# Three sizes of token block in one hybrid decoder step: quarters of 258, a projection moved to the middle, norms from products of x with itself

## The chip, the cores and the metric

One core of a Trainium2 chip runs the whole program. The metric is device time in microseconds (us) of one execution. The engines are PE (TensorE, matmul; PEld is its weight load), DVE (VectorE), ACT (ScalarE), POOL (GpSimd) and SP, whose queue issues every transfer of this kernel.

## The reference

One step of a one-layer hybrid decoder on 1024 prompt tokens and 8 sample tokens, 1032 in all, width 1024, all in float32:

```python
u = rmsnorm(h, norm_mix)
proj = u @ w_in                       # 46 column tiles of 128 and 8 single columns
# RWKV-7 time mixing on one part of proj, gated DeltaNet on another: o_a, o_b
mix = gate_a * (o_a @ w_branch_a) + gate_b * (o_b @ w_branch_b)
h = h + mix @ w_out
u2 = rmsnorm(h, norm_ffn)
h = h + (silu(u2 @ w_ffn_gate) * (u2 @ w_ffn_up)) @ w_ffn_down    # inner width 2816
h = h + sigmoid(rmsnorm(h, norm_ple) @ w_ple_gate) * (pe @ w_ple_proj)   # pe has width 256
y = rmsnorm(h, norm_final)
```

## The kernel before, in words

Everything lies with channels on the 128 partitions and tokens along the free dimension. A float32 product is made of three float32r products: each operand is split into a high and a low half (`xh`, `xl`, `wh`, `wl`), and high·high, high·low and low·high are summed in PSUM (`products`, line 219; line 75 issues each matmul). `weights` (line 190) loads 128x512 pieces of a weight; ACT writes the high half (line 186) and POOL the low half (line 187). A "product" below is one such matmul instruction on PE.

Tokens are cut into three blocks of 344 (`BW`). The stages in order are:

- **Start** (pool `ld`, lines 291 to 401). It loads x (`xs`), the per-layer embeddings (`pes`) and the weights of the per-layer projection (`wps`). `project(m)` makes the eight tiles of pe @ w_ple_proj (144 products) and stores them to `pp_d`. `sums(g)` squares x on ACT and DVE, adds on DVE and POOL and sums over partitions with a float32 product against ones; `inv_rms` (line 269) takes the diagonal, runs a reciprocal square root of 12 small DVE instructions (`rsq`, line 237) and spreads the result R with a float32 product; `scale(g, R)` multiplies `xs` by R and splits it into `xh`, `xl`. PE's order here is the order of the code.
- **The input projection and the two recurrences**. `stream` (line 407) yields the products of the input projection one by one, and `order` (line 112) weaves the recurrences' instructions between them by a model clock.
- **Branches** `wa` and `wb` (lines 1429 to 1461), then the output projection `wo` of the mixer in two parts t: t = 0 is two blocks of 344 tokens, t = 1 two of 172 (`QB`, line 1436). Each result is added to x (tile `H`), stored to `h_d` and squared (`square`, line 1465).
- **mixes(t)** (line 1489) scales H by R (line 1497) and makes seven sums of quarters of the normed input, each split into halves (`ms` line 1507, `xh` line 1509, `xl` line 1510), as the Strassen scheme of the feed-forward needs them.
- **strassen** (line 1543): 22 calls, each with seven products of weight sums, every one on both token parts: 84 matmuls of 344 columns and 84 of 172 a call. After every second pair of calls (one call gives two tiles of gate or up) the down projection `wd` (line 1648) adds to h, which is read from and written back to `h_d`.
- **The end**: gate of the embedding, final norm, store of y, in blocks of 384, 384 and 264 tokens (`EB`).

PSUM has six banks for such accumulators (`acc`), taken in turn. Outside the start and `order`, a scheduler places instructions on every engine by priority; each engine then runs its own list in that order, and SP issues its transfers in order.

Of the kernel before, what the change touches and what calls it, by code (L numbers as in the profile page):

```python
# [58 lines left out]
def hybrid(ctx, tc, a, o):  # L59
# [159 lines left out]
    def products(wh, wl, nk, xh, xl, evac, blocks=range(NBLK), new=None, t0=0):  # L219
        tc.cur_priority += LATER  # L220
        for b in blocks:
            c = cols(b)
            if new:
                new.append(new.pop(0))
                ps = new[-1]()
            else:
                banks.append(banks.pop(0))
                ps = banks[-1].tile([P, width(c)], F32, tag="acc", name="acc")
# [40 lines left out]
    def inv_rms(R, ps, pl_, newps):  # L269
# [7 lines left out]
        tt(e[:, :n], ps, idr[:, :n], MULT)  # L277
        if n >= 2 * P:
            V.tensor_reduce(r[:, 0, 0:2], e[:, 0:2 * P].rearrange("p (i t) -> p i t", t=P), AX.X, ADD)
        for i, c in enumerate(parts):  # L280
            if n < 2 * P or i > 1:
                V.tensor_reduce(r[:, 0, i:i + 1], e[:, c], AX.X, ADD)
# [7 lines left out]

    with tc.tile_pool(name="ld", bufs=1, side="right", reuse_waits="tile") as ld, \
            tc.manual_schedule(engines={mybir.EngineType.PE}):
        xs = ld.tile([P, KT, TOK], F32, name="xs")
        pes = ld.tile([P, 2, TOK], F32, name="pes")
        wps = ld.tile([P, 16, P], F32, name="wps")
        wph, wpl = (ld.tile([P, 16, P], F32R, name=x) for x in ("wph", "wpl"))
        ph, pl = (ld.tile([P, 2, TOK], F32R, name=x) for x in ("ph", "pl"))

        def acc():
            return psd.tile([P, BW], F32, tag="acc", name="acc")  # L300

        spare = [acc, acc, lambda: st1([P, BW]), lambda: psp.tile([P, BW], F32, tag="zp", name="zp")]

        def load_w(m):
            SP.dma_start(wps[:, 2 * m:2 * m + 8].rearrange("p (m k) c -> p m k c", k=2),
                         a["wpp"][m:m + 4].rearrange("m p k c -> p m k c"))

        def load_x(b):
            SP.dma_start(xs[:, :, cols(b)], a["xT"][:, :, cols(b)].rearrange("k p t -> p k t"))
# [4 lines left out]
        load_x(0)  # L314
        load_w(4)
        SP.dma_start(cs, a["const"])
        load_x(1)
        SP.dma_start(vec, a["vec"])
        load_x(2)
        idr = diagonal(ld, BW)  # L320

        own = ld.tile([P, BW], F32, name="own")
        pv = [pes[:, k, cols(b)] for k in range(2) for b in range(NBLK)]
        wv = wps.rearrange("p m c -> p (m c)")
        wv = [wv[:, i * BW:i * BW + BW] for i in range(5)]

        def sums(g):

            sq = (pv + [own], wv + [own], pv)[g]
            for k in range(KT):  # L330
                x, y = xs[:, k, cols(g)], sq[k if k < 4 else 4 + k % (len(sq) - 4)]
                if g == 0 and k in (1, 3, 5):
                    tt(y, x, x, MULT)
                else:
                    act(y, x, AF.Square)
                if k >= 4:
                    (gtt if g or k == 6 else tt)(sq[k - 4], sq[k - 4], y, ADD)
            for k in range(2):
                (gtt if g else tt)(sq[k], sq[k], sq[k + 2], ADD)
            ps = ct([P, BW])  # L340
            for k in range(2):
                mm(ps, ones, sq[k], start=(k == 0), stop=(k == 1))
            return ps

        def inv(g, ps):
            R = ld.tile([P, BW], F32, tag="R0", name="R0", bufs=2)
            tc.cur_priority -= 2 * LATER
            inv_rms(R, ps, ld, ft)
            tc.cur_priority += 2 * LATER
            return R  # L350

        def scale(g, R):
            c = cols(g)
            for k in range(KT):
                (gtt if k % 2 else tt)(xs[:, k, c], xs[:, k, c], R, MULT)
                split(xs[:, k, c], vc("nmix", k), xh[k][:, c], xl[k][:, c])

        def project(m):
            po = ld.tile([P, TOK], F32, tag="po", name="po", bufs=4)

            def evac(b, ps):
                tc.cur_priority -= 3 * LATER
                if b == 1:
                    V.tensor_copy(po[:, cols(b)], ps)
                else:
# [1149 lines left out]
    for t in range(2):  # L1515
# [14 lines left out]
        if t:  # L1530
            astk.close()
# [226 lines left out]
```

## Time and profile before

| what | us |
|---|---|
| timed runs, median of 3 (lowest to highest) | 2151.99 (2151.53 to 2152.81) |
| the profiled execution's own time | 2146.48 |
| its span | 2144.7 |
| PE busy in the span | 2003.7 (93%) |
| DVE, ACT, POOL busy | 1334.3 (62%), 843.2 (39%), 1049.6 (49%) |

PE is busy for nearly all of the span, but matmuls overlap in this profile, so busy says little of the rate: what a product costs is read from the distance between the starts of two neighbours.

### The profile page before, as it was taken

How to read it: one execution, taken by the hardware profiler on the slowest of the kernel's cores; microseconds unless marked ns; L12 is line 12 of the kernel's file. 1: busy time of each engine (PE TensorE's matmuls, PEld its weight loads, DVE VectorE, ACT ScalarE, POOL GpSimd, SP SyncE). 2: the span in 40 equal slices, each digit the busy share in tenths (PEclk: the TensorE clock that was granted, in tenths of full speed). 3: DMA queues.
4: the chain of work that ended last, by engine and by line, in shares of the span. 5: the costliest groups of instructions: out<-in, count | busy, mean ns of one | idle time of the engine just before them, and what ended most of it. 6: DMA issues, size and time to landing. Idle time of an engine off the chain costs nothing.

```text
span 2144.7 us, 40063 instructions
## 1 busy us (share of the span) xinstructions
PE 2003.7 (93%) x14676; PEld 1877.2 (88%) x14676; DVE 1334.3 (62%) x3240; ACT 843.2 (39%) x2068; POOL 1049.6 (49%) x1142
## 2 busy tenths in 40 slices
PE   6998999998999979998899969999999999999996
PEld 5987878777788869898899869999999999999995
DVE  8359766898898279456461785543554535445767
ACT  4333353555554332257232442332413324234532
POOL 5356463566573245730165774544525345354722
PEclk8999999999999999899899969999999999999998
DMA  6334332242343425553555305325143251422322
GB/s 231 119 102 121 112 111 78 92 131 86 102 142 105 133 87 154 164 142 109 189 151 161 110 21 170 107 81 177 45 151 101 69 179 50 140 94 71 124 71 95
DMA packets 214846, 250.86 MB, mean 117 GB/s; under 512 B 47832, under 2 KB 171624, under 8 KB 214648
## 3 DMA queue, kind: packets, MB, share of 16 engines
q1 hardware_dynamic: 214648, 248.29, 37.8%
q8 instruction: 115, 1.88, 0.4%
q14 instruction: 83, 0.68, 0.1%
HBM read 170.82 MB, written 77.40 MB: 116 GB/s over the span
## 4 chain that ended last, share of the span: by engine, by line
PE 68%; DVE 20%; DMA 3%; issue 3%; ACT 3%; POOL 3%; SPq 0%; DVEq 0%; POOLq 0%; ACTq 0%
PE acc L75 59%; PE f L75 3%; PE c L75 2%; DVE GM L738 1%; DVE inv L774 1%; PE zp L75 1%; PE f L79 1%; DVE inv L775 1%; PE s L75 1%; PE x L75 1%; DVE inv L776 1%; DVE L L627 1%; DVE LB L762 1%; DVE H L1497 1%; DMA a<-h_d 1%
## 5 line engine op out<-in xcount | busy, mean ns | idle before, releaser
L75 PE MATMUL acc<-xh,wh 128*128 128x344 f32 (+2 forms) x2360 | 753.1, 320 | 10.5 <-ACT wh L186 6.1
L75 PE MATMUL acc<-xl,wh 128*128 128x344 f32 (+2 forms) x2360 | 751.3, 319 | 6.6 <-DVE xl L1510 6.4
L75 PE MATMUL acc<-xh,wl 128*128 128x344 f32 (+1 forms) x2336 | 746.0, 320 | 1.3 <-POOL wl L187 1.3
L187 POOL TENSOR_TENSOR wl<-ws,wh 128x512 fp32r<-128x512 f32 (+1 forms) x248 | 321.1, 1297 | 463.5 <-ACT wh L186 433.1
L75 PEld LDWEIGHTS acc<-xh,wh 128*128 128x128 f32 (+1 forms) x2360 | 456.1, 193 | 19.1 <-ACT wh L186 6.8
L75 PEld LDWEIGHTS acc<-xl,wh 128*128 128x128 f32 (+1 forms) x2360 | 456.0, 193 | 15.0 <-DVE xl L1510 7.7
L75 PEld LDWEIGHTS acc<-xh,wl 128*128 128x128 f32 x2336 | 453.9, 194 | 7.2 <-POOL wl L187 1.8
L186 ACT ACTIVATE wh<-ws 128x512 fp32r<-128x512 f32 (+1 forms) x248 | 153.7, 622 | 248.5 <-PE acc L75 213.5
L187 POOL TENSOR_TENSOR wl<-s,wh 128x512 fp32r<-128x512 f32 x110 | 142.9, 1300 | 160.9 <-ACT wh L186 160.7
L75 PE MATMUL acc<-hidh,wh 128*128 128x344 f32 x528 | 168.3, 320 | 2.7 <-DVE a L1642 2.6
L75 PE MATMUL acc<-hidl,wh 128*128 128x344 f32 x528 | 169.1, 321 | 0.0
L75 PE MATMUL acc<-hidh,wl 128*128 128x344 f32 x528 | 168.2, 320 | 0.0
L1642 DVE TENSOR_TENSOR a<-a,acc 128x344 f32<-128x344 f32 x120 | 60.8, 511 | 134.0 <-PE acc L75 75.0
L186 ACT ACTIVATE wh<-s 128x512 fp32r<-128x512 f32 x110 | 68.9, 627 | 130.0 <-PE acc L75 110.5
L75 PEld LDWEIGHTS acc<-hidh,wh 128*128 128x128 f32 x528 | 99.0, 188 | 3.6 <-DVE a L1642 3.2
L1600 POOL TENSOR_TENSOR s<-ws 128x512 f32<-128x512 f32 x66 | 86.3, 1307 | 32.5 <-DMA ws<-in_wg 13.7
L75 PEld LDWEIGHTS acc<-hidh,wl 128*128 128x128 f32 x528 | 99.2, 188 | 0.0
L75 PEld LDWEIGHTS acc<-hidl,wh 128*128 128x128 f32 x528 | 99.1, 188 | 0.0
L493 POOL TENSOR_TENSOR cy<-cy,cu 128x344 f32<-128x344 f32 x72 | 69.4, 964 | 50.7 <-ACT cu L492 44.7
L75 PE MATMUL acc<-mxh,wl 128*128 128x344 f32 (+1 forms) x256 | 76.4, 298 | 0.9 <-POOL wl L187 0.9
L1622 DVE TENSOR_TENSOR y<-y,sg 128x344 f32<-128x344 f32 x88 | 75.2, 854 | 3.0
L75 PE MATMUL acc<-mxl,wh 128*128 128x344 f32 (+1 forms) x256 | 76.4, 298 | 0.0
(494 smaller groups left out, 4048.7 us busy)
## 6 DMA issues: line engine op xcount, KB each, us to landing
ws<-in_win SPq DMA_DIRECT2D x92, 256.0 KB, 3.2
a<-h_d SPq DMA_DIRECT2D x120, 172.0 KB, 2.7
h_d<-a SPq DMA_DIRECT2D x120, 172.0 KB, 2.7
pa_d<-gs SPq DMA_DIRECT2D x90, 172.0 KB, 2.1
ws<-in_wg SPq DMA_DIRECT2D x44, 256.0 KB, 2.9
ws<-in_wu SPq DMA_DIRECT2D x44, 256.0 KB, 2.8
ws<-in_wd SPq DMA_DIRECT2D x40, 256.0 KB, 2.6
gate_d<-gs SPq DMA_DIRECT2D x48, 172.0 KB, 2.2
```

The costliest lines, as they stand in the source:

```text
L75: last[0] = TE.matmul(out, w, x, start=start, stop=stop).ins
L79: last[0] = TE.transpose(out, x, ident).ins
L186: act(h, s, AF.Copy)
L187: (eng or gtt)(l, s, h.bitcast(F32), SUB)
L493: gtt(y, y, u, ADD)
L627: V.tensor_tensor_scan(L[:, c * C:c * C + C], ones[:, 0:C], L[:, c * C:c * C + C], 0.0, MULT, ADD)
L738: stt(GM[:, 2 * (c + j) + h], ps[h][:, j], cvf[:, cg, h:h + 1], rwmask, MULT, MULT)
L762: V.transpose(LB[0:32, i0:i0 + 16], G2[:, :, i0:i0 + 16].rearrange("p b i -> p i b"))
L774: tt(u[:, :i], XB[:, :i, :i], LB[:, 16 + i:17 + i, 16:16 + i].to_broadcast([P, i, i]), MULT)
L1600: e(s, A_[p], A_[q], op)
L1622: tt(y, y, sg[i][:, c], MULT)
L1642: tt(y, y, ps, ADD)
```

## The change

Three edits go together. (1) The second half of the layer works on four equal quarters of 258 tokens (`QW`) in place of two blocks of 344 and two of 172: `wb`, `wo`, `mixes` and all Strassen products. (2) The per-layer projection leaves the start and is made after the second part of `wo`, with weights from the common weight path, its embeddings loaded through tile `a`, and each 128x344 result stored on its own from a tile `po` with two buffers. (3) The sums of squares at the start come from float32 products of x with itself (`gram`: a 128x128 block per 128 tokens, of which the diagonal is used). The code of the start stands after `stream` now, so that it can issue the first 144 products of the input projection itself. Pools are placed anew for all this.

```diff
-    def inv_rms(R, ps, pl_, newps):
+    def inv_rms(R, ps, pl_, newps, grams=False):
...
+        if grams:
+            V.memset(r[:, 0], 1.0)
+            for i, c in enumerate(parts):
+                w = slice(0, width(c))
+                tt(e[w, c], ps[w, c], idr[w, c], MULT)
+                V.tensor_reduce(r[w, 0, i:i + 1], e[w, c], AX.X, ADD)
...
-        load_w(0)
-        for b in range(NBLK):
-            SP.dma_start(pes[:, :, cols(b)], a["peT"][:, :, cols(b)].rearrange("k p t -> p k t"))
         load_x(0)
-        load_w(4)
         SP.dma_start(cs, a["const"])
...
+        def gram(g, ps):
+
+            for t0 in range(0, BW, P):
+                w = min(P, BW - t0)
+                for k in range(KT):
+                    x = xs[:, k, g * BW + t0:g * BW + t0 + w]
+                    mm(ps[:w, t0:t0 + w], x, x, start=(k == 0), stop=(k == KT - 1))
+            return ps
...
+        s0 = gram(0, ct([P, BW]))
+        s1 = gram(1, ct([P, BW]))
+        scale(0, inv(0, s0))
+        dense_some(3 * KT)
+        s2 = gram(2, st1([P, BW]))
+        R = inv(1, s1)
+        dense_some(3 * KT)
+        scale(1, R)
+        R = inv(2, s2)
+        dense_some(6 * KT)
+        scale(2, R)
+        dense_some(6 * KT)
...
-    QB = [slice(0, BW), slice(BW, 2 * BW), slice(2 * BW, 5 * BW // 2), slice(5 * BW // 2, TOK)]
-    NT_ = [2 * BW, BW]
+    QW, HW = TOK // 4, TOK // 2
+    QB = [slice(i * QW, i * QW + QW) for i in range(4)]
...
-        dense(a["wb"][m], HB, obh, obl, evac)
+        dense(a["wb"][m], HB, obh, obl, evac, QB)
...
+    mixer_out(0)
+    m0stk.close()
...
+    XM[0] = mixes(xa, 0)
+    for k in range(2):
+        for b in range(NBLK):
+            y = tile("a")
+            SP.dma_start(y, a["peT"][k, :, cols(b)])
+            split(y, None, ph[k][:, cols(b)], pl[k][:, cols(b)])
+    mixer_out(1)
...
+    XM[1] = mixes(xb, 1)
...
+    for m in range(KT):
+        def evac(b, ps, m=m):
+            y = hq[1].tile([P, BW], F32, tag="po", name="po", bufs=2)
+            act(y, ps, AF.Copy)
+            SP.dma_start(pp_d[m, :, cols(b)], y)
+        dense(a["wpp"][m], 2, ph, pl, evac)
...
-            ps = banks[-1].tile([P, width(QB[2 * t])], F32, tag="acc", name="acc")
+            ps = banks[-1].tile([P, QW], F32, tag="acc", name="acc")
```

Three places in the engines' lists show what moved. The first is PE at the very start. Before, PE's list there holds the per-layer projection (`ph`, `pl` on `wph`, `wpl`) with the sums over partitions (`c<-pes,cs`) between:

```order
L75 MATMUL acc_232<-ph_130,wpl_129 128x344
L75 MATMUL c_255<-pes_126,cs_75 128x344 x2
L75 MATMUL acc_259<-ph_130,wph_128 128x344
L75 MATMUL acc_259<-pl_131,wph_128 128x344
L75 MATMUL acc_259<-ph_130,wpl_129 128x344
```

In the change PE's list begins with the products of x with itself (`c<-xs`, `s<-xs`), and the second R (`f_339`) stands behind 24 products of the input projection and the third set of such products:

```order
L75 MATMUL c_138<-xs_125 128x128 x16
L75 MATMUL c_138<-xs_125 88x88 x8
L75 MATMUL c_163<-xs_125 128x128 x16
L75 MATMUL c_163<-xs_125 88x88 x8
L75 MATMUL f_213<-nre_189,cs_75 128x344
L75 MATMUL acc_264<-xh0_101,wh_242 128x344
...
L75 MATMUL acc_264<-xh7_108,wl_249 128x344
L75 MATMUL s_289<-xs_125 128x128 x16
L75 MATMUL s_289<-xs_125 88x88 x8
L75 MATMUL f_339<-nre_315,cs_75 128x344
L75 MATMUL acc_345<-xh0_101,wh_254 128x344
```

So the 144 projection products are gone from here, 72 float32 products came, and input-projection products stand between the norms.

The second place is PE where the mixer's output projection ends. Before, the first Strassen product (`xh00`) follows its last product (`mxh17`) at once:

```order
L75 MATMUL acc_14466<-mxl17_12547,wh_14406 128x172
L75 MATMUL acc_14466<-mxh17_12531,wl_14407 128x172
L75 MATMUL acc_14675<-xh00_13750,wh_14671 128x344
L75 MATMUL acc_14675<-xl00_13757,wh_14671 128x344
L75 MATMUL acc_14675<-xh00_13750,wl_14672 128x344
```

In the change all 144 projection products (`ph`, `pl`) stand between them, and the sums and spreads of the second part's norm (`f<-c`, `f<-nre`) stand among these, 9, 69 and 120 of them in:

```order
L75 MATMUL acc_14456<-mxh17_12322,wl_14396 128x258
L75 MATMUL acc_14648<-ph0_13711,wh_14644 128x344
...
L75 MATMUL f_14430<-c_14428,cs_75 128x258
L75 MATMUL acc_14658<-ph1_13712,wh_14644 128x344
...
L75 MATMUL f_14453<-nre_14433,cs_75 128x258
L75 MATMUL f_14487<-c_14485,cs_75 128x258
L75 MATMUL acc_14776<-ph1_13712,wh_14752 128x344
...
L75 MATMUL acc_14920<-ph1_13712,wl_14897 128x344
L75 MATMUL acc_14944<-xh00_13715,wh_14940 128x258
```

The third place is POOL in the same stretch of the change: the low halves of the first Strassen call's later weights (`wl<-s`) stand behind the first pieces of mixes(1), which need the second part's R (`H10`, `H12` are the scaled tiles):

```order
L187 TENSOR_TENSOR wl_15027<-s_15024,wh_15026 128x512
L1456 TENSOR_TENSOR xl11_14527<-H10_13702,xh11_14520 128x258
L1561 TENSOR_TENSOR s_15069<-ws_14936,ws_14932 128x512
L1456 TENSOR_TENSOR xl11_14527<-H12_13704,xh11_14520 128x258
L187 TENSOR_TENSOR wl_15050<-s_15047,wh_15049 128x512
L1453 TENSOR_TENSOR ms_14545<-H11_13703,H15_13707 128x258
```

From the end of the start stage to the branch products PE's list is the same before and in the change, instruction for instruction.

## Rows read from the trace of the kernel before

**Rows 1.** The profile's page: engines (busy us, share, instructions), TensorE's granted clock in 40 slices, and the chain that ended last, by engine and by line.

```profile
PE 2003.7 (93%) x14676; PEld 1877.2 (88%) x14676; DVE 1334.3 (62%) x3240; ACT 843.2 (39%) x2068; POOL 1049.6 (49%) x1142
...
PEclk8999999999999999899899969999999999999998
...
PE 68%; DVE 20%; DMA 3%; issue 3%; ACT 3%; POOL 3%; SPq 0%; DVEq 0%; POOLq 0%; ACTq 0%
PE acc L75 59%; PE f L75 3%; PE c L75 2%; DVE GM L738 1%; DVE inv L774 1%; PE zp L75 1%; PE f L79 1%; DVE inv L775 1%; PE s L75 1%; PE x L75 1%; DVE inv L776 1%; DVE L L627 1%; DVE LB L762 1%; DVE H L1497 1%; DMA a<-h_d 1%
```

**Rows 2.** Busy time by stage: stretch, its length, busy time and instructions of PE, PEld, DVE, ACT, POOL, then the granted clock (1.00 is 2.4 GHz, 0.50 is 1.2 GHz), DMA share and GB/s. In order: start, input projection with recurrences and `wa`, `wb`, `wo` t = 0, `wo` t = 1, the first two Strassen calls and first `wd`, the other 20 calls with `wd`, the end.

```profile
0.00:59.08 59.08, 36.20 (x160) 31.45 (x161) 51.04 (x98) 30.15 (x67) 31.43 (x36) 0.85 0.60 210
59.08:1074.40 1015.32, 944.23 (x7563) 834.58 (x7563) 701.04 (x1984) 450.51 (x1212) 472.99 (x643) 0.97 0.40 121
1074.40:1119.73 45.33, 45.33 (x291) 45.33 (x289) 29.08 (x46) 15.20 (x31) 34.23 (x31) 1.00 0.48 140
1119.73:1181.60 61.87, 61.87 (x397) 61.67 (x395) 11.17 (x22) 19.41 (x35) 33.29 (x30) 1.00 0.54 162
1181.60:1226.45 44.85, 43.95 (x384) 43.19 (x382) 37.57 (x67) 16.00 (x36) 34.71 (x30) 1.00 0.40 114
1226.45:1344.40 117.95, 93.54 (x515) 87.73 (x513) 81.66 (x161) 44.20 (x109) 77.17 (x81) 0.80 0.33 101
1344.40:2022.50 678.10, 678.10 (x4778) 678.10 (x4779) 336.17 (x666) 229.65 (x503) 322.18 (x255) 1.00 0.34 106
2022.50:2144.70 122.20, 100.47 (x602) 95.10 (x600) 86.55 (x202) 38.09 (x77) 43.59 (x39) 0.93 0.28 90
```

**Rows 3.** PE's instructions in order of time (start us, duration us, engine, line, operation, tiles, shape), first and last of a run: one Strassen round of 24 products begins at 1499.99 with 172 columns, and the next at 1503.22; 1500.07 to 1501.19 is eleven products of 172 columns; 1501.49 to 1503.06 is eleven of 344; 2096.56 to 2098.62 is eighteen of 264 in the end stage.

```profile
1499.99 0.24 PE L75 MATMUL acc<-xh,wh 128*128 128x172 f32 x1
1500.07 0.28 PE L75 MATMUL acc<-xl,wh 128*128 128x172 f32 x1
...
1501.19 0.28 PE L75 MATMUL acc<-xh,wl 128*128 128x172 f32 x1
...
1501.49 0.32 PE L75 MATMUL acc<-xl,wh 128*128 128x344 f32 x1
...
1503.06 0.32 PE L75 MATMUL acc<-xh,wl 128*128 128x344 f32 x1
1503.22 0.24 PE L75 MATMUL acc<-xh,wh 128*128 128x172 f32 x1
...
2096.56 0.28 PE L75 MATMUL acc<-uxh,wh 128*128 128x264 f32 x1
...
2098.62 0.28 PE L75 MATMUL acc<-uxh,wl 128*128 128x264 f32 x1
```

**Rows 4.** The chain that ended last, in order of time (start us, us, what): its longest piece.

```profile
1344.37 678.10 PE acc L75 x4776
```

**Rows 5.** PE in order of time: the first product of `wo` t = 0 and the first of t = 1.

```profile
1119.73 0.32 PE L75 MATMUL acc<-mxh,wh 128*128 128x344 f32 x1
...
1180.15 0.24 PE L75 MATMUL acc<-mxh,wh 128*128 128x172 f32 x1
```

**Rows 6.** The chain that ended last, at the start: x arriving, the first sum of squares' product, and the scaling of a block (`xs`, then the low halves `xl`).

```profile
2.79 8.86 DMA xs<-in_xT
...
19.22 0.86 PE c L75 x2
...
43.20 1.71 DVE xs L355 x4
...
45.33 5.23 DVE xl L254 x8
```

**Rows 7.** PE's groups by form from 0 to 100 us: the products of the input projection (count, busy us, mean ns of one, idle before).

```profile
L75 PE MATMUL acc<-xh,wh 128*128 128x344 f32 x84 | 27.4, 326 | 0.0
L75 PE MATMUL acc<-xl,wh 128*128 128x344 f32 x83 | 27.3, 329 | 0.0
...
L75 PE MATMUL acc<-xh,wl 128*128 128x344 f32 x83 | 26.9, 325 | 0.0
```

**Rows 8.** PE in order of time: two neighbouring runs of float32 products of 128 columns, eight instructions (four products) each.

```profile
942.33 1.06 PE L75 MATMUL x<-S,kc 128*128 128x128 f32 x8
943.22 1.06 PE L75 MATMUL o<-S,q 128*128 128x128 f32 x8
```

**Rows 9.** DVE in order of time at the start: two of the small instructions of the reciprocal square root, about one us apart.

```profile
23.62 0.17 DVE L245 SCALAR_TENSOR_TENSOR nrr<-nrr 128x3 f32<-128x3 f32 x1
...
24.82 0.83 DVE L245 SCALAR_TENSOR_TENSOR nrr<-nrr 128x3 f32<-128x3 f32 x1
```

**Rows 10.** DVE and PE in order of time after the mixer: the scaling of H in mixes(0) and in mixes(1), the last spread of the second part's R (with the idle time before it), and the first product of `wd`.

```profile
1199.01 12.63 DVE L1497 SCALAR_TENSOR_TENSOR H<-H,vec,R 128x688 f32<-128x688 f32 x8
...
1264.62 4.87 DVE L1497 SCALAR_TENSOR_TENSOR H<-H,vec,R 128x344 f32<-128x344 f32 x8 [0.78 <-ACT R L289]
...
1263.29 0.94 PE L75 MATMUL f<-nre,cs 128*128 128x172 f32 x2 [4.68 <-DVE nre L286]
...
1313.02 0.35 PE L75 MATMUL acc<-hidh,wh 128*128 128x344 f32 x1
```

**Rows 11.** ACT in order of time: the copy of one projection result; and the page's transfers: a store of a 128x344 tile (count, KB, us from issue to landing).

```profile
17.42 0.46 ACT L366 ACTIVATE po<-acc 128x344 f32<-128x344 f32 x1 [1.43 <-PE acc L75]
...
pa_d<-gs SPq DMA_DIRECT2D x90, 172.0 KB, 2.1
```

More of the change, by code (lines that the diff above doesn't have):

```diff
@@ L217, in hybrid, with products @@
     banks = [psd]
-    def products(wh, wl, nk, xh, xl, evac, blocks=range(NBLK), new=None, t0=0):
+    def products(wh, wl, nk, xh, xl, evac, blocks=range(NBLK), t0=0):
         tc.cur_priority += LATER
@@ L222, in products @@
             c = cols(b)
[L223 to L228, printed above, removed]
+            banks.append(banks.pop(0))
+            ps = banks[-1].tile([P, width(c)], F32, tag="acc", name="acc")
             for k in range(nk):
@@ L462, in stream, with kvr, load_x, inv @@
                 yield from product(ti, *w, b)
+    def kvr(f):
+        return [4 + f, 8 + f, f]
+    jobs = [12, *kvr(0), 13, *kvr(1), *kvr(2), 18, 19, "b", *kvr(3), 20, 21, 14, 15, 16, 17, 22, 23, 24, 25, 26, 27, 28, 29]
+    dense_in = stream(jobs + list(range(30, 46)))
+    with tc.tile_pool(name="ld", bufs=1, side="right", reuse_waits="tile") as ld, \
+            tc.manual_schedule(engines={mybir.EngineType.PE}):
+        xs = ld.tile([P, KT, TOK], F32, name="xs")
+        def load_x(b):
+            for k in range(0, KT, 4):
+                SP.dma_start(xs[:, k:k + 4, cols(b)], a["xT"][k:k + 4, :, cols(b)].rearrange("k p t -> p k t"))
+        load_x(0)
+        SP.dma_start(cs, a["const"])
+        SP.dma_start(vec, a["vec"])
+        load_x(1)
+        load_x(2)
+        idr = diagonal(ld, BW)
+        def gram(g, ps):
[5 more added lines that the diff above has]
+            return ps
+        def inv(g, ps):
+            R = ld.tile([P, BW], F32, tag="R0", name="R0", bufs=2)
+            tc.cur_priority -= 2 * LATER
+            inv_rms(R, ps, ld, ft, True)
+            tc.cur_priority += 2 * LATER
+            return R
+        def scale(g, R):
+            c = cols(g)
+            for k in range(KT):
+                (gtt if k % 2 else tt)(xs[:, k, c], xs[:, k, c], R, MULT)
+                split(xs[:, k, c], vc("nmix", k), xh[k][:, c], xl[k][:, c])
+        def dense_some(n):
+            for _ in range(n):
+                next(dense_in)
+        s0 = gram(0, ct([P, BW]))
[10 more added lines that the diff above has]
+        dense_some(6 * KT)
+    w0h, a0h, kah, ka1 = vx[:, 0:4], vx[:, 4:8], vx[:, 8:12], vx[:, 12:16]
+    ts(w0h, vc("w0", 0, 4), 0.5, None, MULT)
+    ts(a0h, vc("a0", 0, 4), 0.5, None, MULT)
+    ts(kah, vc("ka", 0, 4), 0.5, None, MULT)
+    ts(ka1, vc("ka", 0, 4), -0.5, 1.0, MULT, ADD)
     def conv(ci):
@@ L1469, in square @@
             return
-        d = tile("c", width(c))
+        d = newd(width(c))
         act(d, src, AF.Square)
@@ L1512, in mixes, with mixer_out @@
         return hi, lo
-    XM = []
-    for t in range(2):
-        qw = width(QB[2 * t])
-        sq = [hq.tile([P, BW], F32, tag=f"sq{i}", name="sq")[:, :qw] for i in range(2)]
+    def mixer_out(t):
+        sq = [hq[t].tile([P, QW], F32, tag=f"sq{i}", name="sq") for i in range(2)]
         for m in range(KT):
             def evac(c, ps, m=m):
-                i = int(c.start > QB[2 * t].start)
-                x = tile("a")[:, :qw]
+                i = c.start // QW % 2
+                x = tile("a")[:, :QW]
                 SP.dma_start(x, a["xT"][m, :, c])
@@ L1555, in new @@
             def new(tag):
-                return sp.tile([P, BW], F32, tag=tag, name=tag)[:, :ps.shape[1]]
+                return sp.tile([P, QW], F32, tag=tag, name=tag)
             if n == 0:
@@ L1624, in hybrid @@
             strassen(a["wg"], f0 + j, gate, f0 + j == 0)
+            if f0 + j == 0:
+                pbs.close()
+                hp = pool(hstk, "hid")
+                hh, hl = pair(hp, "hid", 4)
+                tmp = pool(hstk, "tf", 2)
+                depth[0] = 5
             strassen(a["wu"], f0 + j, up)
@@ L1632, in hybrid @@
             ux = pool(ctx, "ux", 1, "right")
-            uh, ul = pair(ux, "ux", KT)
+            uh, ul = ([xb.tile([P, TOK], F32R, tag=f"x{q}{k}", name=f"ux{q}{k}") for k in range(KT - 1)] for q in "hl")
+            for x, q in ((uh, "h"), (ul, "l")):
+                x.append(ux.tile([P, TOK], F32R, name=f"ux{q}"))
             ac = ux.tile([P, TOK], F32, name="ac")
```

196 lines of the change are left out of this document (47 added, 149 removed).

## The prediction

> **What bounds the kernel now.** I read the page first [rows 1]: PE is busy for 93% of the span and two thirds of the chain that ended last is PE. A busy PE says nothing of its rate, so the next view is the table by stage [rows 2]. In 678 us of Strassen and down projection PE never stops, at full clock, with DVE, ACT and POOL at 50%, 34% and 48%; in the chain these 678 us are one piece [rows 4]. There the rate of PE alone sets the time. Two stretches are of another kind: the start, where DVE is busy for 51 of 59 us and PE for 36, and the 118 us behind the mixer, where PE is busy for 93.5 at a clock of 0.80. There something is late for PE.
>
> What a product costs is the distance between starts [rows 3]: ten steps of 172 columns take 1.12 us, so 112 ns each; ten of 344 take 1.57, so 157 ns; seventeen of 264 take 2.06, so 121 ns. Half the columns cost 71%, so a 172-column product pays for a floor. A round of twelve of each takes 3.23 us [rows 3].
>
> **Part 1: quarters of 258.** The columns stay the same; 258 has no row of its own. From 264 and 344, 80 columns are 36 ns, so six columns less than 264 are 2.7 ns and 258 columns should follow every 118.3 ns. The bounds are the floor (112) and the 264 row itself (121). A round of 24 takes 24 x 0.1183 = 2.84 us in place of 3.23, a call of seven rounds 19.9 in place of 22.6. For the 20 calls in the saturated stretch that is 20 x 2.73 = **55 us** gained (bounds 46 and 76 from 121 and 112 ns). What hides the other engines' work remains: even in 622 us in place of 678 DVE would be at 54%.
>
> `wo` t = 0 runs from 1119.73 to 1180.15 [rows 5], 60.4 us for 384 products at 157 ns. 384 of 118.3 ns are 45.4: **15 us** gained (14 to 17). Its second part grows (384 x 112 ns to 45.4); that is counted in part 2's stretch.
>
> `wb` has 288 products of 344 before, 384 of 258 after: 45.2 against 45.4 us. Its POOL, at 34 of 45 us [rows 2], gets one more fixed cost per weight tile, and its tile `c` has two buffers for a chain over DVE, POOL, ACT and DVE that now comes every 1.42 us. I take a **loss of 2** (0 to 6).
>
> The Trainium skill (TensorE: Matmul & The Clock Gate, section Back-to-back issue gap) gives a warm distance of columns / 2.4 GHz + 2.5 ns: 110 ns for 258 columns. It would give 146 for 344, where the trace has 157 [rows 3], so I go by the trace. By an estimate from that section of the Trainium skill, part 1 would gain about 30 us more (3744 products x 8.3 ns), which comes near rival C.
>
> **Part 2: the projection behind the mixer.** It takes 144 products from the start and adds 144 x 157 ns = 22.6 us of PE behind `wo`, with 16 weight pieces for ACT and POOL, 6 loads through tile `a`, 24 copies on ACT and 24 stores. Before, the stretch from the second part of `wo` to the first `wd` product, 1180.15 to 1313.02, takes 132.9 us [rows 5, 10]. Without waits it would now take 45.4 for `wo`, 22.6 for the projection and 2 x 19.9 for two Strassen calls: 108 us. So the projection has room, if it falls where PE waits now.
>
> It does only in part. The second part's R needs two float32 sums and spreads that stand among the projection products, the last behind 120 of 144, so R comes some 21 us after `wo`. Then DVE scales eight tiles of 516 columns, 4.87 x 516 / 344 = 7 us [rows 10], or 9.5 by the first part's row (12.63 x 516 / 688), where POOL is busy too. On POOL the low halves of the first call's last weights stand behind the first pieces of mixes(1) and wait with them for the scaled tiles; PE gets to them later than that, so they cost nothing. POOL then makes half of mixes(1) between the weights' low halves. It is the engine that fills up here, 77 of 118 us before [rows 2] and now with half again as many columns in mixes(1); I put 33 to 40 us on it. On `wo`'s start as zero: R at 67, last piece of mixes(1) at 107 to 110, then one whole call of 20: 128 us, 20 of them waits. That is a **gain of 5** (from a loss of 12 to a gain of 20, the last if POOL keeps up).
>
> The tile `po` has two buffers; a copy of 0.46 and a store of 2.1 [rows 11] make one result every 1.3 to 1.4 us, where PE makes one every 0.94 (six products). Six banks soften it, and the rest falls into the wait for mixes(1): late there is POOL, not PE. If that cover is gone, it costs up to 24 x 0.45 = 11 us.
>
> **Part 3: the start.** Before, the products of the input projection begin at 59.1 us, but 250 are done by 100 us [rows 7], so PE's effective start is 100 - 250 x 0.157 = 60.8. What makes it late is on the chain [rows 6]: x lands at 11.65, behind 1.6 MB of embeddings and weights; the sum reaches PE at 19.2; x is first scaled at 43.2. In between DVE copies projection results and runs small instructions of 0.17 us that take 0.83 while POOL works [rows 9].
>
> After, x is first in the queue. By the share of bytes (1.4 of 3.0 MB in 11.65 us, with the first latency) block 0 lands at about 6.5. A set of 24 products of x with itself costs 24 x 0.222 = 5.3 us at full clock ([rows 8]: eight instructions, four products, in 0.89), twice that at half. With part of it at half clock set 0 ends at 13.5, set 1 at 19; R of block 0 (DVE, 5 us) lies beside set 1 and comes at 20. Scaling and eight low halves (1.7 + 5.2, [rows 6]) end at 28, set 2 at 34, R of block 1 at 36, its scaling and R of block 2 at 49.5. By then 48 input products are done and nothing holds the rest: start 49.5 - 48 x 0.157 = 42, and 2 more for low clock: 44. **Gain 17** (8 if all sets run at half clock, and all small instructions at 0.83; 26 if none do). Behind it PE's list is the same, so the recurrences shift as a whole.
>
> **Sum.** 55 + 15 - 2 + 5 + 17 = 90 us. The profiled execution took 2146.5, so 2056.5 by its own time. The timed runs' median lies 5.5 above it; I subtract from that: 2152.0 - 90 = **2062 us**.
>
> **Rivals.**
>
> B, the move takes the place of the wait: the projection is fully visible, `po` holds it to the pace of its stores, and mixes(1) still ends late. Then the stretch loses 15 in place of winning 5, with PE at half clock in the gaps, as its 0.80 shows [rows 2]: 2082. For it: POOL's list and the late R. Against: that stretch has 45 us beyond its products' time now (132.9 - 384 x 0.112 - 2 x 22.6), and the move needs 22.6.
>
> C, 258 columns come down to the floor that 172 shows, 112 ns: the 20 calls gain 76 in place of 55, the two parts of `wo` 2.4 more each, the first two calls 2: 2062 - 21 - 7 = 2034. For it: 172 and 258 would share one limit. Against: 264 at 121. By the rule of the Trainium skill named in part 1 it would be about the same; the trace at 344 does not agree with that rule.
>
> D, the change doesn't do what it says: a 258-column product costs the mean of the old pair, 134.5 ns. Then Strassen gains nothing, `wo` 106.7 - 768 x 0.1345 = 3, `wb` loses 6, 17 of the start remain, and the stretch behind the mixer comes out even: 2138. Against it stands the 264 row.
>
> E, slower: PE falls to the half clock inside Strassen, because every accumulator is now handed over at one pace of 1.42 us, and an engine behind PE misses it. At half a product takes 0.237 us and a call 39.8 in place of 19.9; 90 us are gone when 4.5 of 22 calls run so, and with six it is 2181. For it: the clock of 0.80 where PE waits now. Against: 1.00 for 678 us with no other engine above 50% [rows 2].
>
> **How the numbers follow.** The forecast gets 0.66, with 2044 to 2082 as its own range from the part bounds. B gets 0.15, C 0.10, D 0.05, E 0.04. The predicted time is the forecast's; 2032 to 2094 takes in B and C and leaves out D, E and the ends of the bounds. About 0.2% (4 us) is what a measurement here can tell from no change. Faster: the forecast, B, C and 0.03 of D, 0.94; same 0.02, the rest of D; slower 0.04, E.
>
> **What would show it.** Right: 258-column products 118 ns apart; the long saturated piece near 622 us at clock 1.00; input products dense from about 50 us; the products of `ph` running without a gap behind `wo`, then waits on POOL or on mixes(1) in the first call's second half. Wrong: distances of 112 or 134 ns; PE idle before DVE's or ACT's evacuation inside later calls; projection products more than 1.3 us per result; the first input products after 55 us.

## The result, and the profile after

The changed kernel takes **2084.64 us** (median of 4 runs, 2083.20 to 2094.33), the kernel before on the same chip 2152.40 (2151.53 to 2160.09): a ratio of 0.969, 95% interval 0.965 to 0.972. That is 68 us less, where 90 were forecast; 2084.6 lies in the range of 2032 to 2094 and just outside the forecast's own one, 2044 to 2082. The profiled execution took 2085.75, 60.7 less than the 2146.5 of the one before, which lay 5.9 under the median of 2152.40. The terms are therefore compared trace with trace, against 60.7.

From the page of the changed kernel, what answers to [rows 1]:

```profile
span 2084.0 us, 40641 instructions
PE 1943.8 (93%) x14904; PEld 1819.6 (87%) x14904; DVE 1321.5 (63%) x3253; ACT 845.0 (41%) x2069; POOL 1045.1 (50%) x1144
PEclk8999899999999999999899998999999999999998
PE 64%; DVE 21%; DMA 4%; ACT 4%; issue 4%; POOL 3%; SPq 0%; DVEq 0%; POOLq 0%; ACTq 0%
```

The same table by stage as [rows 2], at the changed kernel's own cuts: the start up to the first dense input products, recurrences and `wa`, `wb`, the two parts of `wo`, the stretch up to the end of the first `wd`, the dense Strassen calls, the end. Columns as there.

```profile
core 0: us, PE busy (x) PEld busy (x) DVE busy (x) ACT busy (x) POOL busy (x), PEclk, DMA share, GB/s
0.00:53.02 53.02, 30.40 (x198) 27.94 (x199) 32.65 (x95) 14.75 (x27) 18.66 (x22) 0.82 0.41 141
53.02:1070.53 1017.51, 942.45 (x7514) 833.28 (x7513) 702.60 (x1975) 447.33 (x1207) 473.90 (x643) 0.96 0.40 119
1070.53:1116.45 45.92, 45.92 (x386) 45.92 (x385) 30.77 (x62) 17.01 (x38) 33.70 (x39) 1.00 0.49 138
1116.45:1162.53 46.08, 46.08 (x387) 46.08 (x386) 9.05 (x20) 17.19 (x33) 30.14 (x30) 1.00 0.65 188
1162.53:1212.34 49.81, 48.22 (x396) 47.82 (x395) 38.33 (x78) 22.55 (x54) 35.96 (x36) 1.00 0.55 158
1212.34:1331.61 119.27, 99.13 (x634) 92.63 (x632) 84.53 (x157) 50.20 (x127) 72.19 (x75) 0.93 0.42 132
1331.61:1962.22 630.61, 630.57 (x4800) 630.36 (x4801) 337.81 (x666) 237.20 (x507) 336.43 (x264) 1.00 0.38 117
1962.22:2083.98 121.76, 101.04 (x604) 95.61 (x602) 85.71 (x202) 38.79 (x79) 44.11 (x39) 0.92 0.26 82
```

Laid beside the start times of the same products before, the 60.7 us divide so ("at 100 us" is the start of the 250th input product, 99.95 before and 87.12 after):

| term | forecast | measured | from |
|---|---|---|---|
| start, at 100 us | 17 | 12.8 | 99.95 - 87.12 |
| the same, at the first `wb` product | 17 | 3.9 | 1074.45 - 1070.53 |
| `wb` | -2 | -0.6 | 45.3 to 45.9 |
| `wo`, first part | 15 | 14.3 | 60.4 to 46.1 |
| second part of `wo` to first `wd` product | 5 | -7.1 | 132.9 to 139.9 |
| first group of `wd` | 0 | -2.8 | 26.3 to 29.1 |
| Strassen and `wd` behind it | 55 | 52.3 | 682.9 to 630.6 |
| the end | 0 | 0.7 | 122.4 to 121.8 |

Two terms are far off, and both are stretches in which PE waits: of the start's gain 8.9 us are gone before the recurrences end, and the stretch behind `wo`'s first part lost 10 (with the first `wd`) in place of winning 5. The experiments are for these two, and for what part 1 is worth alone.

### The profile page after: what moved, and what is told of

Read it like the earlier page. It is cut to its first block, busy times and chain, and to the rows that moved or that the text cites. A ratio compares the mean times of both kernels' runs of the same rounds, so it can differ in the third digit from the quotient of the medians.

```text
span 2084.0 us, 40641 instructions
## 1 busy us (share of the span) xinstructions
PE 1943.8 (93%) x14904; PEld 1819.6 (87%) x14904; DVE 1321.5 (63%) x3253; ACT 845.0 (41%) x2069; POOL 1045.1 (50%) x1144
## 4 chain that ended last, share of the span: by engine, by line
PE 64%; DVE 21%; DMA 4%; ACT 4%; issue 4%; POOL 3%; SPq 0%; DVEq 0%; POOLq 0%; ACTq 0%
PE acc L75 54%; PE c L75 3%; PE f L75 3%; DVE GM L685 1%; PE zp L75 1%; DVE inv L721 1%; PE f L79 1%; PE s L75 1%; DVE L L574 1%; PE x L75 1%; DVE H L1443 1%; DMA a<-h_d 1%; DVE inv L722 1%; DVE LB L709 1%; DMA out_gdns<-St 1%
## 5 line engine op out<-in xcount | busy, mean ns | idle before, releaser
L75 PE MATMUL acc<-xh,wh 128*128 128x258 f32 (+2 forms) x2360 | 733.3, 311 | 13.1 <-ACT gs L328 5.7
L75 PE MATMUL acc<-xl,wh 128*128 128x258 f32 (+2 forms) x2360 | 728.0, 309 | 9.7 <-DVE xl L250 5.6
L75 PE MATMUL acc<-xh,wl 128*128 128x258 f32 (+1 forms) x2336 | 722.9, 310 | 0.0
L187 POOL TENSOR_TENSOR wl<-ws,wh 128x512 fp32r<-128x512 f32 (+1 forms) x256 | 334.7, 1309 | 440.2 <-ACT wh L186 408.3
L75 PEld LDWEIGHTS acc<-xh,wh 128*128 128x128 f32 (+1 forms) x2360 | 450.7, 191 | 22.8 <-ACT gs L328 6.0
L75 PEld LDWEIGHTS acc<-xl,wh 128*128 128x128 f32 (+1 forms) x2360 | 451.2, 191 | 18.3 <-DVE xl L250 6.4
L75 PEld LDWEIGHTS acc<-xh,wl 128*128 128x128 f32 x2336 | 448.5, 192 | 5.8 <-POOL wl L187 0.5
L445 POOL TENSOR_TENSOR cy<-cy,cu 128x344 f32<-128x344 f32 x72 | 68.8, 955 | 50.2 <-ACT cu L444 44.1
L75 PE MATMUL acc<-mxh,wh 128*128 128x258 f32 x256 | 72.7, 284 | 0.0
L75 PE MATMUL acc<-mxl,wh 128*128 128x258 f32 x256 | 72.6, 284 | 0.0
L75 PE MATMUL acc<-mxh,wl 128*128 128x258 f32 x256 | 72.2, 282 | 0.0
```

Source lines behind the costliest of these rows:

```text
L75: last[0] = TE.matmul(out, w, x, start=start, stop=stop).ins
L187: (eng or gtt)(l, s, h.bitcast(F32), SUB)
L445: gtt(y, y, u, ADD)
```

## Experiments

**The place where the head start is lost.** Comparing the starts of the same instructions in the two traces shows that it is lost at one spot: PE is 13.6 us ahead of before at 185 us and 4.6 ahead at 260. The first line is PE's longest wait there in the changed kernel, the second that of before (who waits for whom: us in total, times, longest).

```profile
PE acc L75 <- ACT gs L328: 5.7, 1, 5.7
```

```profile
PE acc L75 <- ACT gs L440: 1.5, 1, 1.5
```

ACT's own rows there (start, duration, operation, names; in brackets its idle time and who ended it; `...` where rows are left out), first of the changed kernel, then of the kernel before:

```profile
196.90 0.62 ACT L707 COPY inv<-GM 32x512 f32<-32x512 f32 x1 [4.60 <-DVE inv L741]
197.54 0.63 ACT L586 ACTIVATE d<-KR 128x512 f32<-128x512 f32 x1
198.08 0.61 ACT L186 ACTIVATE wh<-ws 128x512 fp32r<-128x512 f32 x1
198.60 0.61 ACT L586 ACTIVATE d<-KR 128x512 f32<-128x512 f32 x1
202.21 0.23 ACT L623 ACTIVATE Gc<-L 128x16 f32<-128x16 f32 x1 [3.00 <-DVE L L574]
202.35 0.61 ACT L186 ACTIVATE wh<-ws 128x512 fp32r<-128x512 f32 x1
202.87 0.78 ACT L328 ACTIVATE gs<-acc 128x344 f32<-128x344 f32 x2
```

```profile
207.97 0.62 ACT L760 COPY inv<-GM 32x512 f32<-32x512 f32 x1 [3.41 <-DVE inv L794]
208.49 0.44 ACT L440 ACTIVATE gs<-acc 128x344 f32<-128x344 f32 x1
...
211.25 0.43 ACT L440 ACTIVATE gs<-acc 128x344 f32<-128x344 f32 x1
212.83 0.63 ACT L639 ACTIVATE d<-KR 128x512 f32<-128x512 f32 x1 [1.15 <-POOL k L634]
217.75 0.23 ACT L676 ACTIVATE Gc<-L 128x16 f32<-128x16 f32 x1 [4.28 <-DVE L L627]
```

The copies `gs` free the two accumulators of the input projection. Before, both stand ahead of `Gc`, the exponential that needs the last of sixteen scans on DVE. In the changed kernel `Gc` stands first, and PE's accumulators wait behind it for DVE. PE's list is the same in both; ACT's and DVE's are not: the scheduler has placed them otherwise. Then the clock adds its part (windows of the changed kernel, columns as above): it is 0.82 over the wait, 0.50 over the next 7.6 us and 0.59 over the 9 behind them, although PE is busy all through both.

```profile
197.65:203.36 5.71, 0.04 (x2) 0.00 (x1) 5.68 (x12) 2.71 (x7) 2.39 (x4) 0.82 0.03 7
203.36:211.00 7.64, 7.64 (x54) 6.84 (x55) 4.92 (x11) 0.88 (x2) 4.72 (x8) 0.50 0.65 194
211.00:220.00 9.00, 9.00 (x78) 8.57 (x78) 4.25 (x11) 2.84 (x5) 0.59 (x3) 0.59 0.09 27
```

Two runs separate this order from the rival that the recurrences swallow any head start. One holds `Gc` back:

```diff
-        act(Gc, ch(L[:, :T])[:, :, C - 1], AF.Exp)
+        late(act(Gc, ch(L[:, :T])[:, :, C - 1], AF.Exp))
```

> The changed kernel with one line more: the activation that makes Gc is held behind the products issued so far, so that ACT's copies of the accumulators stand ahead of it. Theory A (order): PE's wait of 5.7 us at 197 us and the half clock behind it go, 8 to 9 us, and the head start of 13 us reaches the end of the recurrences as 11 to 13: total 2074 to 2077. Theory B (absorbed): the wait shows up at the next place, total 2083 to 2086.

Measured: 2078.63 us, ratio to before 0.966 (0.962 to 0.969); a little above what was expected, and its interval overlaps the changed kernel's, so the times alone would not carry it. The trace does: the two copies run at 196.57, with no `Gc` ahead, and PE's wait for them is 2.4 us in place of 5.7 (the row of ACT, then PE's wait, as above).

```profile
196.57 0.78 ACT L328 ACTIVATE gs<-acc 128x344 f32<-128x344 f32 x2
```

```profile
PE acc L75 <- ACT gs L328: 2.4, 1, 2.4
```

The other keeps the squares in the new start, on the engines of before. ACT's order at `Gc` is then that of before too:

```diff
...
-                    mm(ps[:w, t0:t0 + w], x, x, start=(k == 0), stop=(k == KT - 1))
...
+            for k in range(KT):
+                x, y = xs[:, k, cols(g)], sq[k if k < 4 else 4 + k % 2]
+                if g == 0 and k in (1, 3, 5):
+                    tt(y, x, x, MULT)
+                else:
+                    act(y, x, AF.Square)
+                if k >= 4:
+                    (gtt if g or k == 6 else tt)(sq[k - 4], sq[k - 4], y, ADD)
...
+            for k in range(2):
+                mm(ps, ones, sq[k], start=(k == 0), stop=(k == 1))
...
```

> The changed kernel, but the mean squares are formed as before (squares on ACT, DVE and POOL, then two products with ones); x is still first in the queue and the projection still behind the mixer. In this kernel ACT's order at the second feature of the recurrences is that of before: the copies of input products (gs) stand ahead of Gc, which waits for sixteen scans on DVE. Theory A (order): the head start of the input products over before, whatever it is (I expect 8 to 11 us), is kept to within 4 us until the end of the recurrences, where the changed kernel kept 4 of 13; total 2078 to 2083. Theory B (the recurrences absorb a head start): 2 to 5 us are left there whatever the start does, and the total is 2084 to 2087.

Measured: 2098.05 us (0.975, 0.971 to 0.979): slower than the changed kernel, which neither theory said. Its head start at 100 us is 6.7, so the products of x with itself are worth 6 us at the start. At the spot of `Gc` theory A holds: 1.5 us lost in place of 9. Behind it another 8.6 went, which theory A excluded. The table below sets this beside all runs, as PE's lead over the profiled execution before (us):

| run | `Gc` | 100 us | 185 | 260 to 300 | first `wb` product |
|---|---|---|---|---|---|
| changed kernel | ahead | 12.8 | 13.6 | 4.6 | 3.9 |
| changed kernel again | ahead | 13.1 | 14.2 | 5.1 | 0.9 |
| without projection | ahead | 11.5 | 12.8 | 3.5 | -8.3 |
| without projection, 2nd | ahead | 12.9 | 14.0 | 4.9 | 6.9 |
| embedding later | ahead | 13.1 | 14.0 | 4.9 | 5.3 |
| mixes on DVE | ahead | 12.6 | 13.3 | 3.3 | 4.4 |
| `Gc` behind | behind | 13.1 | 16.7 | 12.6 | 10.8 |
| products first | behind | 22.8 | 23.9 | 19.8 | 15.9 |
| three places | behind | 22.6 | 25.5 | 22.1 | 6.9 |
| squares kept | behind | 6.7 | 7.1 | 5.6 | -3.0 |
| quarters alone | behind | 0.6 | 0.6 | -0.6 | -14.0 |

Between 185 and 260 the six runs with `Gc` ahead all lose 9.0 to 10.0, the five with it behind 1.2 to 4.1. The difference is the order's price, and it repeats. The one line of `Gc` behind is worth 8.0 at 260 us (12.6 in place of 4.6); 3.1 of that are there at 185 already; the line also holds back an earlier `Gc`, before 140 us. What happens from 260 us on does not go by the kernel: the first six rows have the same instructions up to `wb`, in the same order but for a few neighbours, and between 260 us and there they lose anything from -2.0 to 11.8. The second run of the changed kernel was for this:

> The changed kernel itself, once more, for two things: as the yardstick for the run below on the same chip, and to see how far two executions of one program lie apart in the recurrences. If the 12.7 us by which the changed kernel and the one without the projection differ at the end of the recurrences, with the same instructions up to there, are chance, this profile should show its own value there, somewhere between 1023 and 1036, and the same times as before (within 1 us) up to 220 us, the loss of 9 at 190 to 215 included. Total 2083 to 2087, times the ratio of the chips.

Measured: 2089.47 us, before on that chip 2155.51 (ratio 0.968, 0.965 to 0.972). The lead up to 260 us repeats within 0.6, and at the end of the recurrences it is 3.0 lower. With the other five of the first six rows, which end from -8.3 to 6.9, a profile-to-profile difference of some 10 us in the recurrences is chance. The low time of the profiled execution before may be chance too: on this chip alone eleven runs of it lie from 2149.08 to 2171.17.

**The start.** In the changed kernel the R of block 1 is spread at 40.01, 24 products run, and then PE stands for 7.68 us before the spread of block 2's R, although DVE makes block 1's low halves between 45.3 and 50.2 (start, duration, operation, names, count):

```profile
4.98 12.44 PE L75 MATMUL c<-xs 128*128 128x128 f32 x96 [4.98 <-DMA xs<-in_xT]
22.16 0.65 PE L75 MATMUL acc<-xh,wh 128*128 128x344 f32 x1 [4.13 <-ACT xh L249]
35.19 4.98 PE L75 MATMUL s<-xs 128*128 128x128 f32 x48
40.01 0.78 PE L75 MATMUL f<-nre,cs 128*128 128x344 f32 x2
52.22 1.51 PE L75 MATMUL f<-nre,cs 128*128 128x344 f32 x2 [7.68 <-DVE nre L290]
```

The next run, on top of `Gc` behind, puts all three sets ahead and the third spread behind 48 input products (the line of `Gc` is left out here):

```diff
-        scale(0, inv(0, s0))
-        dense_some(3 * KT)
+        R = inv(0, s0)
         s2 = gram(2, st1([P, BW]))
-        R = inv(1, s1)
-        dense_some(3 * KT)
-        scale(1, R)
+        R1 = inv(1, s1)
+        scale(0, R)
+        dense_some(6 * KT)
         R = inv(2, s2)
+        scale(1, R1)
```

> The kernel with Gc held behind, and at the start all three sets of products of x with itself stand ahead of the input products, and the third spread of R behind 48 of them. The wait of 7.7 us at 44.4 (PE for the R of block 2, whose spread stands in PE's order ahead of block 1's products) should go: theory A: block 1's products start at 43 to 46 in place of 53, the head start over the kernel before is 18 to 21 us at 100 us in place of 13, and as the order at Gc passes it on, the total is 2070 to 2074, against 2078.6 with Gc alone. Theory F (DVE is what is late): DVE's small instructions of the second R ahead of the scaling of block 0 only delay the first product (22.2) by 4 to 6, the head start stays at 12 to 14, total 2077 to 2080.

Measured: 2079.05 us, before on that chip 2157.95 (0.965, 0.961 to 0.968). The lead at 100 us is 22.8, more than expected, although the first product starts at 35.8 in place of 22.2: PE's wait is now one of 13.1 us, ahead of the first product. 15.9 of the lead reach `wb`. So theory A's lead came, but the times do not confirm it: by the ratio this run cannot be told from `Gc` behind alone.

**Part 1 alone.** The kernel before with four quarters; projection and squares stay at the start.

```diff
-    QB = [slice(0, BW), slice(BW, 2 * BW), slice(2 * BW, 5 * BW // 2), slice(5 * BW // 2, TOK)]
-    NT_ = [2 * BW, BW]
+    QW, HW = TOK // 4, TOK // 2
+    QB = [slice(i * QW, i * QW + QW) for i in range(4)]
+    NT_ = [HW, HW]
...
```

> The kernel before with part 1 alone: four quarters of 258 columns in wb, wo and the Strassen calls; the projection and the squares stay at the start. From the two traces, part 1 is 52.0 us in the 20 Strassen calls, 14.4 in wo t = 0, a loss of 0.6 in wb and of about 3 in the second part of wo: together 63, so about 2089 against 2152, with 258-column products 120 ns apart and the start and the recurrences as before. If the parts hinder each other less than that, and the junction behind wo gains here what the projection took from it, it is nearer 2083 and the changed kernel's other two parts are worth nothing or less. If the quarters only pay together with the moved projection, it is above 2100.

Measured: 2094.06 us (0.973, 0.968 to 0.978), 59 less: between the first and the third expectation, nearest the first. By the medians part 1 is seven eighths of the whole change (59 of 68); the two intervals overlap, so what parts 2 and 3 add is not shown. The traces, leaving out the recurrences behind 260 us where chance rules, give them nothing: at 260 us the changed kernel is 5.2 us ahead of the quarters alone, and from `wb` to the end it takes 8.7 more. The stretch from the second part of `wo` to the first `wd` product alone is 130.4 us in the quarters alone, 9.5 less than the changed kernel's.

**The stretch behind the mixer.** Two runs leave the projection out (its 144 products and 16 weight pieces; 24 copies of the embedding are stored instead). In the first the copies came ahead of mixes(0) on ACT, in the second where the projection's copies stood.

```diff
-        def evac(b, ps, m=m):
+        for b in range(NBLK):
...
-            act(y, ps, AF.Copy)
+            act(y, ph[m % 2][:, cols(b)].bitcast(F32), AF.Copy)
             SP.dma_start(pp_d[m, :, cols(b)], y)
-        dense(a["wpp"][m], 2, ph, pl, evac)
```

> The changed kernel without the projection behind the mixer: its 144 products, 16 weight pieces and 8 weight loads are left out, and the 24 tiles that are stored are copies of the embedding instead. Theory C (the late R): with no products ahead of them the two spreads of R come some 10 us after wo instead of 31, mixes(1) ends 15 to 20 us earlier, and the stretch from the second part of wo to the first wd product takes 115 to 122 us in place of 140: total 2060 to 2068. Theory D (POOL): POOL is the limit there, mixes(0) alone keeps it until 1234 us, and the stretch takes 130 to 136: total 2074 to 2080. Fully hidden would be 140 and no change.

> As the run without the projection (its 144 products, 16 weight pieces and 8 weight loads left out, copies of the embedding stored in place of its results), but the 24 copies on ACT now stand among mixes(1), where the projection's copies stood; in the first such run they came ahead of mixes(0), which started at 27.5 us on the zero of wo's second part in place of 22.6. Theory H (the projection is hidden behind mixes): the stretch from the second part of wo to the first wd product takes 136 to 140 us, as with the projection. Theory C (late R by the projection): 115 to 130. In between, at 130 to 136, POOL's 16 weight pieces are what it costs.

Measured: 2086.47 us for the first, with the stretch at 139.9, as with the projection; 2079.06 (one run, before beside it 2160.89) and 136.5 for the second. The R of the second part does not come earlier without the projection: its last spread is 85.7 and 82.6 us behind the start of `wo`'s second part, with it 79.4. The stretch repeats well: in the changed kernel, its second run and the three other runs that leave this stage alone it is 139.8 to 140.2. So 22.6 us of products cost 3.4 us there: nearly all of them are hidden, as theory H has it, and theory C falls.

The other neighbour of R is the embedding: its six loads and splits stand ahead of the second part of `wo`.

```diff
-    for k in range(2):
...
-            split(y, None, ph[k][:, cols(b)], pl[k][:, cols(b)])
+    def load_pe():
+        for k in range(2):
...
+                split(y, None, ph[k][:, cols(b)], pl[k][:, cols(b)])
     mixer_out(1)
+    load_pe()
```

> The changed kernel, but the six loads and splits of the embedding stand behind the second part of wo in the program in place of ahead of it. Theory C (they delay R): the spreads of the first part's R come at 9 and 18 us on the zero of wo's second part, as in the run with the quarters alone, in place of 13 and 22; its scaling and mixes(0) start 4 us earlier, and all behind them too: the stretch from the second part of wo to the first wd product takes 134 to 136 us in place of 140, total 2078 to 2081. Theory D (POOL and DVE are full until R of the second part anyway): the stretch stays at 138 to 141, total 2083 to 2086.

Measured: 2080.45 us (0.965, 0.962 to 0.967) and a stretch of 134.5: theory C's numbers. The first part's spreads come at 9.1 and 17.6 us, mixes(0) starts 4 us earlier. The trace carries this; the ratio's interval overlaps the changed kernel's. This stretch is only 4.1 above that of the quarters alone, with the whole projection in it.

What is left is the size of mixes(1). The windows from the scaling of the second part to its last low half, each cut to within 0.9 us, of the kernel before, the quarters alone and the changed kernel (the first number behind the window is its length; then PE, PEld, DVE, ACT, POOL):

```profile
1263.80:1291.20 27.40, 22.82 (x100) 21.64 (x98) 22.01 (x42) 14.67 (x42) 22.93 (x30) 0.58 0.05 14
```

```profile
1258.00:1296.50 38.50, 24.88 (x147) 23.66 (x147) 29.41 (x42) 17.46 (x45) 30.69 (x33) 0.69 0.15 44
```

```profile
1242.72:1285.60 42.88, 34.51 (x225) 31.71 (x224) 35.21 (x49) 23.70 (x60) 37.49 (x37) 0.84 0.23 74
```

Half of the tokens in place of a third: from the start of the scaling to the end of the last low half, 27.1 us become 38.3 with part 1 alone, and 43.5 beside the projection. The last run asks whether POOL is the limit:

```diff
-                e, e2 = (gtt, tt) if k % 2 else (tt, gtt)
+                e, e2 = (tt, tt) if t else (gtt, tt) if k % 2 else (tt, gtt)
```

> The changed kernel, with all 48 sums and low halves of mixes(1) on DVE; POOL keeps the weights' low halves alone. Theory D (POOL fills up, as the prediction has it): mixes(1), 37 us from the scaling to its last piece, is done in 25 to 30 (48 of 0.41 to 0.5 us), the stretch from the second part of wo to the first wd product takes 128 to 133 us in place of 140, total 2073 to 2079. Theory E (DVE is as full as POOL, and its instructions are slowed by POOL's anyway): 48 pieces of 0.7 to 0.9 us take 40 or more, the stretch 142 to 150, total 2087 to 2095.

Measured: 2084.82 us (0.966, 0.964 to 0.969) and 138.9: neither theory. The same window is 40.8 long, and POOL is free for more than half of it, but DVE is busy for nearly all of it:

```profile
1242.40:1283.20 40.80, 32.07 (x217) 29.32 (x216) 40.53 (x72) 23.79 (x60) 17.62 (x12) 0.92 0.23 77
```

So it is not POOL alone: with POOL's share on DVE, mixes(1) takes 41.2 us in place of 43.5, and DVE is what fills up.

**All three places together**: `Gc` behind, products first, embedding later.

> The changed kernel with Gc held behind the products, the three sets of products of x with itself ahead of the input products, and the loads and splits of the embedding behind the second part of wo. If the three places are independent of each other, 8 to 9 us at Gc, 9 to 10 at the start and 5.4 in the stretch behind wo's first part add up: profile to profile 19 to 24 less than the changed kernel, 2060 to 2068 by its own time. If the recurrences take part of it back, as the run with the three sets first showed it (22.8 us of head start at 100 us, 15.9 at the end), it is 14 to 18: 2067 to 2071. If nothing of it reaches the end it is above 2078.

Measured: 2074.52 us (6 runs, 2063.63 to 2081.61) beside the changed kernel's 2089.47 (6 runs, 2081.33 to 2092.83) on the same chip: 15 less by the medians, which is the second expectation's difference; 0.962 of before (0.958 to 0.965). It is faster than both kernels. The expectation counted profile with profile, and there it is only 8.5 less: the profiled execution, 2079.8 of span, was the longest of the six, and 15 us of its lead went between 260 us and `wb`. The stretch behind the mixer takes 136.8 us, so the later embedding wins 3.1 there in place of 5.4; why is open.

## Why the prediction was right and where it was wrong

**Part 1: right, its price a little low.** Behind the first `wd` the Strassen calls take 80.64 us for four (20.16 each, 19.9 predicted), before 90.42: 9.78 gained for four, 49 for twenty. Another 3.1 come from waits in the first group before (93.9 in place of 90.4). In a row 258 columns follow each other every 118.9 ns, 27 steps in 3.21 us:

```profile
1400.01 0.28 PE L75 MATMUL acc<-xh,wh 128*128 128x258 f32 x1
...
1403.22 0.28 PE L75 MATMUL acc<-xh,wh 128*128 128x258 f32 x1
```

The line through 264 and 344 gave 118.3. Over a call, with the steps from one accumulator to the next, it is 120.0; by that the twenty calls lost 5.7 of the 55, and the waits gave 3.1 back. Rivals C and D are out. The 110 ns by the Trainium skill (TensorE: Matmul & The Clock Gate, section Back-to-back issue gap) were not reached: the trace decides, as it did at 344. That section of the Trainium skill gives the formula for a product on its own, without a budget for its weight load; here every product loads its weights. Rival E did not happen: the 630 us run at clock 1.00. `wo`'s first part (14.3 for 15) and `wb` (-0.6 for -2) are as forecast.

**Part 2: the step that failed is that R comes some 21 us after `wo`, because its sums and spreads stand among the projection products.** On `wo`'s start as zero it came at 79.4 in place of 67: `wo`'s second part took 49.6 us in place of 45.4, and R came 30 us after it, as late or later without the projection. These 12 us are the miss; behind R the forecast holds (60.5 us from R to the first `wd` product, 61 forecast). The rows of PE show a chain in place of the projection, with the row of DVE that makes the second sum's input at the end:

```profile
1216.65 0.70 PE L75 MATMUL f<-c,cs 128*128 128x258 f32 x2 [2.89 <-DVE c L1428]
1231.13 0.70 PE L75 MATMUL f<-nre,cs 128*128 128x258 f32 x2 [2.55 <-DVE nre L290]
1231.67 0.65 PE L75 MATMUL f<-c,cs 128*128 128x258 f32 x2
1241.67 0.60 PE L75 MATMUL f<-nre,cs 128*128 128x258 f32 x2
```

```profile
1218.56 0.50 DVE L1428 TENSOR_TENSOR c<-c,sq 128x258 f32<-128x258 f32 x1 [0.77 <-ACT c L1420]
```

The first spread comes 14.5 us behind its sum: DVE runs the instructions for it among pieces of mixes(0), which last until 72 us on the same zero, and they take 12.1 us from first to last. The second sum's input was ready at 1219.1, but the sum stands behind that spread in PE's list. Its instructions on DVE wait for the last piece of mixes(0) and then take 5.2 us with no such piece between. That this order sets R is read from the trace; no run changes it. The trace before could have warned: with no projection there, R's last spread came 37 us after `wo` [rows 2, 10]. Mixes(1) was sized right (33 to 40, measured 37 behind the scaling), but not POOL alone fills up there: DVE does too. Its growth with the larger second part is a price of part 1, whose stretch won only 2.5 us by itself. The six loads and splits of the embedding, counted but costed at nothing, took 3.1 to 5.4.

`po` did not set a pace of 1.3 to 1.4 us per result. The 24 results take 35.4 us, more than the 1.3 us each that the prediction named as a sign of being wrong, but 13 of the 23 steps from result to result are 0.94 to 0.96, and only 3.2 us are waits for `po`; 5.5 are waits for the sums and spreads of R:

```profile
PE acc L75 <- ACT po L1498: 3.2, 2, 1.6
PE f L75 <- DVE c L1428: 2.9, 1, 2.9
PE f L75 <- DVE nre L290: 2.6, 1, 2.6
```

Rival B's time is near the measured one, but not by its mechanism: its projection was to be fully visible, and 3.4 of 22.6 are.

**Part 3: the start was 4 us short, and the step that failed is "PE's list is the same, so the recurrences shift as a whole".** R of block 1 was ready on DVE at 33.9, before the 36 forecast, but its spread stood behind 24 input products and the third set and ran at 40.0. R of block 2 then came at 52.2 in place of 49.5, and the spread itself and the low clock took the rest: the 250th product is at 87.1, an effective start of 47.9 in place of 44. Then 9.0 us were lost at `Gc`, from 13.6 ahead at 185 us to 4.6 at 260. PE's list is the same; ACT's is not, and that could be read before the run from the order in which the two kernels place `gs` and `Gc`.

**Sum.** 90 - 13.1 (start and recurrences) - 14.9 (stretch and first `wd`) - 2.7 (Strassen) + 1.4 (`wb`, the end and `wo` together) gives the 60.7 of the traces. The runs' medians give 7 more, because the profiled execution before lay 5.9 under its median and that of the changed kernel 1.1 above its own. Part 1 carries the result; parts 2 and 3, forecast at 22, left nothing that can be told from chance. Whether the losses from 260 us on also hold an order's effect stays open: the chance of single executions there is larger than any difference left.

## What to carry to other kernels

A head start on one engine can be lost where another engine's in-order list has changed; compare the lists of the engines that free the bottleneck's buffers, not the bottleneck's own alone. Where a later stage has two parts, making them equal lengthens the second part's preparation (here 27.1 to 38.3 us), so part sizes have a price on both sides. To place work into a wait costs little when what ends the wait runs on other engines (3.4 us for 144 products here), but the small steps that come with it (six loads and splits, 3.1 to 5.4 us) can cost as much.

## What was unexpected of the hardware

PE can stay at the low clock while the profile shows it busy without a gap, for a length that differs from one execution to the next. The window 890 to 935 us of the quarters alone, the first run without the projection, and `Gc` behind (columns as above):

```profile
890.00:935.00 45.00, 45.00 (x419) 36.88 (x415) 7.07 (x23) 10.16 (x18) 23.37 (x31) 0.63 0.47 123
```

```profile
890.00:935.00 45.00, 45.00 (x496) 37.82 (x496) 10.00 (x30) 12.65 (x25) 27.82 (x37) 0.82 0.62 147
```

```profile
890.00:935.00 45.00, 43.74 (x435) 40.40 (x432) 17.33 (x61) 19.70 (x65) 25.52 (x33) 1.00 0.61 179
```

The granted clock is 0.63, 0.82 and 1.00, with PE busy for 45.0, 45.0 and 43.7 of 45 us. With 0.63 in the first, most of the window is at the lower level of 1.2 GHz, and between 865 and 950 us that run lost 10.1 us of its lead, while `Gc` behind won 4.8. The changed kernel, with the same instructions there as the run without the projection, has 0.96 in this window with PE busy for 43.2 us.

The cost of a product with its weights is not a line in its columns: 172 take 112 ns, 258 take 118.9, 264 take 121, 344 take 157, each at clock 1.00.
